# Sums and squares of the last row group in PSUM, with refitted last load sizes, in a streamed sum of squared differences

## The chip, the cores and the metric

One core of a Trainium2 chip. The metric is the device time in microseconds (us) of one execution; inputs lie in HBM, the result goes back to HBM. Most executions of one kernel agree within about 0.3%. A span is the length of one profiled execution; times inside a trace count from its start, which is the issue of the first load.

Three engines matter. SyncE (SP) issues the transfers (DMA), VectorE (DVE) subtracts, ScalarE (ACT) squares and sums. SBUF and PSUM are two memories of the core; the program chooses for each tensor in which of them it lies (`alloc_sbuf_tensor`, `alloc_psum_tensor`).

## The reference

```python
x, y: float32 [1024, 4096]
out = np.sum((x - y) ** 2, axis=-1)        # float32 [1024]
```

Each of the 128 partitions holds 8 consecutive rows, so row group r (called row r) is columns 4096 r to 4096 r + 4095 of a 128 x 32768 matrix. 33.55 MB are read once.

## The kernel before: the parts concerned

The widths of the loads (`xw` of X, `yw` of Y), all issued by SyncE, in columns; each Y load is issued after the X loads that it needs:

```python
xw = [4096, 12288, 8192, 5472, 1280, 960, 320, 160]
yw = [16256, 8192, 2624, 2784, 1344, 480, 480, 288]
late, last = 128, 192        # last: the end of row 7; late: the last 128 columns of row 3, loaded last of all
halved = (1, 2, 3, 4)        # these Y loads are computed in two halves per row
```

For each piece VectorE subtracts in place and ScalarE squares in place; `accum_out` gives a second ScalarE instruction, READ_ACCUMULATOR, which writes the piece's sum into one column of `parts` (for a row in one piece, straight into `results`):

```python
def sub(c0, c1):
    a = X[:, home(c0, c1)]
    nc.vector.tensor_sub(out=a, in0=a, in1=Y[:, home(c0, c1)]).then_inc(diffs, 1)

def square(c0, c1, acc):
    a = X[:, home(c0, c1)]
    nc.scalar.wait_ge(diffs, n["diffs"])
    nc.scalar.activation(out=a, in_=a, func=Square, accum_out=acc).then_inc(acts, 1)
```

A row in several pieces is completed by a VectorE reduction of its columns of `parts`. The last load (the end of row 3) is squared and summed on VectorE itself, while ScalarE does the last piece of row 7. In the traces this sum is CUSTOM_DVE_ANT_0, followed by VectorE's own DVE_READ_ACCUMULATOR2_ANT. The code (cut):

```python
for j, (c0, c1) in enumerate(ys):
    final = j == len(ys) - 1
    wait_loaded(c1, landed_y[j][1])
    for piece in pieces_of(j, c0, c1):
        sub(*piece)
        if final:
            # tensor_tensor_reduce on VectorE, its initial value the first part of row 3
            ...
        square(*piece, where[piece])
        ...
    if j == 4:
        for r in (4, 5, 6):
            complete(r)
complete(7)                   # VectorE waits for ScalarE's last sum, reduces 8 numbers
nc.sync.wait_ge(sums, n["sums"])
nc.sync.dma_start(out=ov, in_=results)
```

Of the kernel before, what the change touches and what calls it, by code (L numbers as in the profile page):

```python
# [47 lines left out]
def kernel(tc, x, y, axis, out):  # L48
    nc = tc.nc
    P = nc.NUM_PARTITIONS  # L50
    F32 = mybir.dt.float32
    Square = mybir.ActivationFunctionType.Square
# [3 lines left out]
    R = B // P  # L56
# [11 lines left out]
    results = nc.alloc_sbuf_tensor("results", [P, R], F32).ap()  # L68



    xw = [4096, 12288, 8192, 5472, 1280, 960, 320, 160]
    yw = [16256, 8192, 2624, 2784, 1344, 480, 480, 288]
    late, last = 128, 192
    LATE = 3
    halved = (1, 2, 3, 4)
    cut = (LATE + 1) * D - late
# [16 lines left out]
    acts = prog.semaphore("acts")  # L94
# [3 lines left out]
    def home(c0, c1):  # L98
        h0 = c0 % H
        return slice(h0, h0 + c1 - c0)  # L100
# [25 lines left out]
    row_parts = [[] for _ in range(R)]  # L126
# [16 lines left out]
    parts, where = None, {}  # L143
    total = sum(len(p) for p in row_parts if len(p) > 1)
    parts = nc.alloc_sbuf_tensor("parts", [P, total], F32).ap()
    k = 0
    for r, p in enumerate(row_parts):
        for piece in p:
            where[piece] = parts[:, k : k + 1] if len(p) > 1 else results[:, r : r + 1]
            k += len(p) > 1  # L150
    first = {}
    k = 0
    for r, p in enumerate(row_parts):
        if len(p) > 1:
            first[r] = k
            k += len(p)

    def parts_of(r, m):
        return parts[:, first[r] : first[r] + m]

    seen_x = [0]

# [15 lines left out]
    def square(c0, c1, acc):  # L178
        a = X[:, home(c0, c1)]
        nc.scalar.wait_ge(diffs, n["diffs"])  # L180
        nc.scalar.activation(out=a, in_=a, func=Square, accum_out=acc).then_inc(acts, 1)  # L181
        n["acts"] += 1

    squared = {}
# [1 line left out]
    def complete(r):  # L186
        nc.vector.wait_ge(acts, squared[row_parts[r][-1]])
        nc.vector.tensor_reduce(  # L188
            out=results[:, r : r + 1],
            in_=parts_of(r, len(row_parts[r])),  # L190
            axis=mybir.AxisListType.X,
            op=add,
        ).then_inc(sums, 1)
        n["sums"] += 1
# [6 lines that stand above are left out]
            r = piece[0] // D  # L201
            if final:
                nc.vector.wait_ge(diffs, n["diffs"])
                nc.vector.tensor_tensor_reduce(  # L204
                    out=Y[:, home(*piece)],
                    in0=X[:, home(*piece)],
                    in1=X[:, home(*piece)],
                    scale=1.0,
                    scalar=parts_of(r, 1),
                    op0=mult,  # L210
                    op1=add,
                    accum_out=results[:, r : r + 1],
                ).then_inc(sums, 1)
                n["sums"] += 1
                continue
            square(*piece, where[piece])
            squared[piece] = n["acts"]
            if r in (0, 1):

                nc.sync.wait_ge(acts, n["acts"])  # L220
                while todo and todo[0][5] <= H + (r + 1) * D:
                    load(*todo.pop(0))
                if r == 1:
                    while todo:
                        load(*todo.pop(0))
# [43 lines left out]
```

## Time and profile before

| | before |
|---|---|
| time, median of the first 3 runs (range) | 84.03 us (84.0 to 84.2) |
| span of the profiled run | 82.6 us |
| DMA engines busy | 95.9% of the span |
| DVE / ACT busy | 45% / 40% |
| last reduction starts / ends | 80.99 / 81.15 us |

How to read it: the 16 DMA engines are busy for nearly the whole span and data arrives until about 79.85 us, so the time is the stream plus a tail. The lines stand in the prediction below. In what follows "landing" is the time of the last of the 16 semaphore updates that the trace records for a load. The load before the last (192 columns before, 160 after) landed at 80.052 us before.

### The profile page before, as it was taken

The page shows a single profiled execution, that of the slowest core. Times are in us where ns is not written, and L with a number is a line of the kernel's source. Part 1 is how long each engine was busy: PE and PEld are TensorE (multiplying, and loading weights), DVE is VectorE, ACT ScalarE, POOL GpSimd, SP SyncE. Part 2 cuts the span into 40 slices and gives each one's busy share as a digit, 9 for nine tenths or more (in the row PEclk, how much of TensorE's full clock was granted, in tenths as well). Part 3 has the DMA queues.
Part 4 walks back from the last instruction along what each step waited for, and adds up shares of the span by engine and source line. Part 5 has one row for each costly group of instructions (what it writes and reads, how often), then busy time and mean ns, then how long its engine had stood idle before and what let it go on. Part 6 is the DMA issues. An engine that isn't in the chain of part 4 may idle for free.

```text
span 82.6 us, 136 instructions
## 1 busy us (share of the span) xinstructions
DVE 36.8 (45%) x27; ACT 33.4 (40%) x41; POOL 0.2 (0%) x4
## 2 busy tenths in 40 slices
DVE  0000000000000000000299999999189996989992
ACT  3300000000000000000000979889896999899991
POOL 0000000000000000000000000000000000000000
DMA  5998998888999991999599699969979799999960
GB/s 127 389 500 381 595 547 381 381 381 381 504 504 504 504 504 63 441 504 504 254 508 508 286 476 508 476 286 508 423 339 509 339 437 440 426 402 416 395 220 2
DMA packets 2736, 33.56 MB, mean 406 GB/s; under 512 B 432, under 2 KB 1328, under 8 KB 1712
## 3 DMA queue, kind: packets, MB, share of 16 engines
q1 hardware_dynamic: 2736, 33.56, 95.9%
HBM read 33.55 MB, written 0.00 MB: 406 GB/s over the span
## 4 chain that ended last, share of the span: by engine, by line
DMA 63%; SPq 16%; DVE 12%; ACT 4%; issue 1%
DMA Y<-in_y_dram 63%; SPq L108 16%; DVE X L175 11%; ACT X L181 4%; DVE Y L204 0%; DVE results L188 0%; SPq L220 0%; DVE results L204 0%
## 5 line engine op out<-in xcount | busy, mean ns | idle before, releaser
L175 DVE TENSOR_TENSOR X<-X,Y 128x2048 f32<-128x2048 f32 (+10 forms) x21 | 36.2, 1780 | 44.3 <-DMA Y<-in_y_dram 44.3
L181 ACT ACTIVATE X<-X 128x2048 f32<-128x2048 f32 (+9 forms) x20 | 31.2, 1559 | 46.1 <-DVE X L175 46.0
L181 ACT ACTIVATION_READ_ACCUMULATOR X<-X 128x1 f32 x20 | 3.7, 186 | 0.0
L181 ACT ACT_TABLE_LOAD x1 | 1.3, 1283 | 1.4 <-PEq L19 1.4
L188 DVE TENSOR_REDUCE results<-parts 128x1 f32<-128x2 f32 (+2 forms) x4 | 0.4, 152 | 0.0
L204 DVE CUSTOM_DVE_ANT_0 Y<-X,parts 128x128 f32<-128x128 f32 x1 | 0.4, 352 | 0.0
L250 POOL MEMSET const-bfloat16-1.0<- 128x1 bf16 x1 | 0.1, 101 | 0.0
L250 POOL MEMSET const-uint8-127<- 128x1 uint8 x1 | 0.1, 101 | 0.0
L250 POOL MEMSET const-float32-0.0<- 128x1 f32 x1 | 0.1, 98 | 0.2 <-issue 0.2
L250 POOL MEMSET const-float32-1.0<- 128x1 f32 x1 | 0.1, 98 | 0.0
L204 DVE DVE_READ_ACCUMULATOR2_ANT results<- 128x1 f32 x1 | 0.1, 83 | 0.0
## 6 DMA issues: line engine op xcount, KB each, us to landing
Y<-in_y_dram SPq DMA_DIRECT2D x1, 8128.0 KB, 39.0
X<-in_x_dram SPq DMA_DIRECT2D x1, 6144.0 KB, 20.2
X<-in_x_dram SPq DMA_DIRECT2D x1, 4096.0 KB, 48.3
Y<-in_y_dram SPq DMA_DIRECT2D x1, 4096.0 KB, 57.5
X<-in_x_dram SPq DMA_DIRECT2D x1, 2736.0 KB, 13.3
X<-in_x_dram SPq DMA_DIRECT2D x1, 2048.0 KB, 7.1
Y<-in_y_dram SPq DMA_DIRECT2D x1, 1392.0 KB, 19.0
Y<-in_y_dram SPq DMA_DIRECT2D x1, 1312.0 KB, 16.1
```

The source lines that it names most:

```text
L108: nc.sync.dma_start(out=dst[:, home(c0, c1)], in_=src[:, c0:c1]).then_inc(sem, 16)
L175: nc.vector.tensor_sub(out=a, in0=a, in1=Y[:, home(c0, c1)]).then_inc(diffs, 1)
L181: nc.scalar.activation(out=a, in_=a, func=Square, accum_out=acc).then_inc(acts, 1)
L188: nc.vector.tensor_reduce(out=results[:, r : r + 1], in_=parts_of(r, len(row_parts[r])), axis=mybir.AxisListType.X, op=add,).then_inc(sums, 1)
L204: nc.vector.tensor_tensor_reduce(out=Y[:, home(*piece)], in0=X[:, home(*piece)], in1=X[:, home(*piece)], scale=1.0, scalar=parts_of(r, 1), ...
L250: nc = _bacc.Bacc("TRN2", target_bir_lowering=False, num_devices=1)
```

## The change

Intent: ScalarE writes row 7's squares and sums to PSUM instead of SBUF, to make each piece take less time, and the last loads are cut again to fit. The diff (cut):

```diff
-    xw = [4096, 12288, 8192, 5472, 1280, 960, 320, 160]
-    yw = [16256, 8192, 2624, 2784, 1344, 480, 480, 288]
-    late, last = 128, 192
+    xw = [4096, 12288, 8192, 5472, 1344, 640, 576, 160]
+    yw = [16256, 8192, 2656, 2816, 1344, 640, 288, 288]
+    late, last = 128, 160
...
+    last_parts = nc.alloc_psum_tensor("last_parts", [P, 512], F32).ap()
+    last_squares = nc.alloc_psum_tensor("last_squares", [P, 7 * 512], F32).ap()
+    squares_at = {}
+    # from the last piece of row 7 backwards, as many as fit
+    for piece in reversed(row_parts[-1]):
+        w = piece[1] - piece[0]
+        if k + w > 7 * 512:
+            break
+        squares_at[piece] = last_squares[:, k : k + w]
+        k += w
...
     def parts_of(r, m):
-        return parts[:, first[r] : first[r] + m]
+        home_of = last_parts if r == R - 1 else parts
+        return home_of[:, first[r] : first[r] + m]
...
-        nc.scalar.activation(out=a, in_=a, func=Square, accum_out=acc).then_inc(acts, 1)
+        to = squares_at.get((c0, c1), a)
+        nc.scalar.activation(out=to, in_=a, func=Square, accum_out=acc).then_inc(acts, 1)
```

Row 7 has 8 pieces on either side: 640, 672, 672, 672, 480, 480, 288, 192 before; 672, 704, 672, 672, 640, 288, 288, 160 after. All 8 sums go to PSUM, and the squares of the last 7 pieces. PSUM is touched by ScalarE alone until VectorE's reduction, which waits for ScalarE's last sum.

More of the change, by code (lines that the diff above doesn't have):

```diff
@@ L145 @@
     parts = nc.alloc_sbuf_tensor("parts", [P, total], F32).ap()
+    last_parts = nc.alloc_psum_tensor("last_parts", [P, 512], F32).ap()
+    last_squares = nc.alloc_psum_tensor("last_squares", [P, 7 * 512], F32).ap()
+    squares_at = {}
     k = 0
-    for r, p in enumerate(row_parts):
-        for piece in p:
-            where[piece] = parts[:, k : k + 1] if len(p) > 1 else results[:, r : r + 1]
-            k += len(p) > 1
+    for piece in reversed(row_parts[-1]):
[4 more added lines that the diff above has]
+        k += w
     first = {}
@@ L154 @@
         if len(p) > 1:
-            first[r] = k
-            k += len(p)
+            first[r] = 0 if r == R - 1 else k
+            k += 0 if r == R - 1 else len(p)
     def parts_of(r, m):
-        return parts[:, first[r] : first[r] + m]
+        home_of = last_parts if r == R - 1 else parts
+        return home_of[:, first[r] : first[r] + m]
+    for r, p in enumerate(row_parts):
+        for k, piece in enumerate(p):
+            where[piece] = parts_of(r, len(p))[:, k : k + 1] if len(p) > 1 else results[:, r : r + 1]
     seen_x = [0]
```

## The prediction

> **What bounds the kernel now.** I read the page first: the DMA row of the slices, the queue share and the chain that ended last.
>
> ```profile
> DVE 36.8 (45%) x27; ACT 33.4 (40%) x41; POOL 0.2 (0%) x4
> DMA  5998998888999991999599699969979799999960
> q1 hardware_dynamic: 2736, 33.56, 95.9%
> DMA 63%; SPq 16%; DVE 12%; ACT 4%; issue 1%
> ```
>
> Both compute engines are idle more than half of the span; the 16 DMA engines are busy for 95.9% of it, and the row of slices runs on into slice 39. (The single 1 there is bookkeeping of long packets, not a hole: by the list of DMA issues and the chain, the first long X load lands at 1.43 + 20.2 = 21.6 us and the first long Y load, 8128 KB = 8.32 MB, at 40.84 us, which is 433 GB/s without a pause.) The 33.55 MB that must be read is the same in both kernels. So the kernel is the stream of loads plus a tail, and only the tail can move. The table by stretches shows where the stream stops (columns: stretch, its length, DVE busy, ACT busy, POOL busy, clock, DMA share, GB/s):
>
> ```profile
> 74.00:76.00 2.00, 2.00 (x4) 2.00 (x7) 0.00 (x0) 1.00 1.01 417
> 76.00:78.00 2.00, 2.00 (x4) 2.00 (x5) 0.00 (x0) 1.00 1.02 405
> 79.60:79.70 0.10, 0.10 (x1) 0.10 (x1) 0.00 (x0) 1.00 1.05 305
> 79.80:79.90 0.10, 0.10 (x1) 0.10 (x1) 0.00 (x0) 1.00 0.08 16
> 79.90:80.00 0.10, 0.10 (x1) 0.10 (x2) 0.00 (x0) 1.00 0.00 0
> ```
>
> Data ends near 79.85 us; VectorE (DVE) and ScalarE (ACT) have been full since 74. The three have been balanced against each other. Next the chain in order of time (columns: start, length, what):
>
> ```profile
> 66.94 13.12 DMA Y<-in_y_dram
> 80.08 0.57 DVE X L175 x2
> 80.67 0.35 DVE Y L204
> 81.03 0.12 DVE results L188
> ```
>
> The timeline (columns: start, length, engine, line, operation, destination and sources):
>
> ```profile
> 79.47 0.59 ACT L181 ACTIVATE X<-X 128x480 f32<-128x480 f32 x1
> 79.58 1.06 DVE L175 TENSOR_TENSOR X<-X,Y 128x288 f32<-128x288 f32 x3 [0.15 <-DMA Y<-in_y_dram]
> 80.08 0.44 ACT L181 ACTIVATE X<-X 128x288 f32<-128x288 f32 x1
> 80.42 0.19 ACT L181 ACTIVATION_READ_ACCUMULATOR X<-X 128x1 f32 x1
> 80.52 0.35 ACT L181 ACTIVATE X<-X 128x192 f32<-128x192 f32 x1
> 80.77 0.19 ACT L181 ACTIVATION_READ_ACCUMULATOR X<-X 128x1 f32 x1
> 80.95 0.08 DVE L204 DVE_READ_ACCUMULATOR2_ANT results<- 128x1 f32 x1
> 80.99 0.16 DVE L188 TENSOR_REDUCE results<-parts 128x1 f32<-128x8 f32 x1
> 81.18 0.35 SPq L232 DMA_DIRECT2D out_dram<-results  x1
> ```
>
> Two paths meet at the last reduction of row 7. DVE: the 192-column load lands at 80.05, subtraction at 80.08, the 128 late columns of row 3 are subtracted and summed by 80.95, their accumulator is read by 81.03. ACT: its last piece can only start at 80.52, because the pieces before it fill it, and its accumulator is out at 80.96. The reduction starts at 80.99, within 0.04 us of both, ends at 81.15, and the store takes the rest up to 82.6. The whole tail after the last-but-one landing, up to the start of the reduction, is 80.99 - 80.05 = 0.94 us. The measured time, 84.03 us, is the span plus about 1.4 us.
>
> **What the Trainium skill says.** "PSUM — Partial Sum Buffer" (Specifications, engine access) says ScalarE writes PSUM faster than SBUF. "Perfetto Trace Analysis" (Optimizing Scalar/DVE Operations) gives sizes: about 93 ns of access overhead for ScalarE on SBUF against 51 on PSUM, and about 60 against 125 for VectorE. The before trace has no PSUM operand, so it can't confirm either. "ScalarE: Activation LUTs" (What ACT_TABLE_LOAD costs) gives 186 ns + 0.833 ns per column for an ACTIVATE with immediate operands; the trace agrees: 192 columns took 347 ns (formula 346), 672 took 754 (746). "DMA: Bandwidth & Descriptors" (Where 436 GB/s comes from) puts the ceiling at 435 GB/s; 433 above agrees, so the stream has nothing left to give.
>
> **The change part by part.** By the order of instructions, every engine has as many instructions on both sides: 20 ACTIVATEs, 21 subtractions, 18 loads and the store. No wait is added or removed.
>
> *Loads.* As many descriptors (18 loads of 128 rows) and the same bytes, so the fixed cost per packet is paid equally often and the stream ends where it did, 79.85 us. The last two Y loads (160 and 128 columns instead of 192 and 128) still land about 80.05 and 80.25. Effect: 0, with phase noise of maybe 0.1 us.
>
> *DVE's last pieces.* In the trace the 192-column subtraction holds DVE for 0.28 us before the next (80.08 to 80.36, the start of a 285 ns instruction that ends at 80.65), that is 0.20 for 192 columns at 1.04 ns (slope from 2048 and 4096 columns: (4421 - 2287)/2048) and 0.08 fixed. With 160 columns it starts the next at 80.08 + 0.167 + 0.08 = 80.33, after the landing at 80.25, so row 3's end comes 0.033 us sooner: its sum starts near 80.64 and lets go of DVE near 80.95 to 80.96.
>
> *ACT's shorter pieces.* From start to start a piece costs ACT its columns at 0.833 plus about 0.20 us (672 columns: 78.11 to 78.88 = 0.77; 480: 78.88 to 79.47 = 0.59). The new cut gives ACT of row 7 two 288s, a 160, a 640 and 704 in place of 480, 480, 288, 192 and 640. I walked this queue with landings shifted by the columns that follow. With the old 0.20 it would start the last 160 at about 80.73 and have its sum out near 81.14, that is 0.18 later than now: **the new sizes alone would lose**. With 0.04 us less per piece (estimate, 93 - 51 ns, from the page "Perfetto Trace Analysis") it reaches the 640 before its subtraction is done, starts it at 79.10, then 79.80, 80.20 and 80.60, and is out near 80.93. With 0.08 (both instructions of a piece gaining) 80.83. So PSUM pays for the new cut; it does not add a gain of its own beyond the DVE bound of 80.95.
>
> *The reduction.* It now reads its 8 numbers from PSUM: +0.065 us at most (estimate, 125 - 60 ns, same page) on the path that ends last; the before kernel's reduction took 0.16.
>
> Sum on the path: start of the reduction 80.99 to about 80.96 (-0.03), its length +0.00 to +0.065. Net -0.03 to +0.03 us of 84.03: nothing that a median of three can hold.
>
> **The rivals.** (1) *ACT was the real bound of the tail* and is relieved by much more than I took: then the end follows DVE, and cannot be earlier than the last landing plus two subtractions and the sum; at best -0.1 us, 83.93. For: ACT has no gap from 74 to 81. Against: DVE is equally full and ends within 0.04 us of it. (2) *PSUM writes save ACT no time between pieces* (only the acknowledgement that already overlaps the next instruction gets shorter): then the finer cut makes ACT late, +0.1 to +0.18 us, 84.15 to 84.2. For: READ_ACCUMULATOR's 186 ns already overlap the next ACTIVATE by half (80.42 + 0.19 against a start at 80.52). Against: the cut was evidently fitted to something shorter. (3) *The stream shifts*: the new starting columns change how rows are cut, for 0.1 us either way. Before and after have about equally many such small loads, so I give it noise only. (4) Collisions in PSUM: ACT alone writes there, and DVE reads only after ACT's last semaphore, so none.
>
> **Range and chances.** Centre: 84.03 - 0.03 to + 0.03, pulled down slightly by rival 1, gives 83.98. The three old runs span 84.0 to 84.2, so medians wander by some 0.1; with the +0.18 of rival 2 and stream noise of 0.1 I take 83.78 to 84.2. A 2% gain is 1.68 us, more than the 0.94 us tail that could be touched, so faster gets 0.01; a 2% loss needs the stream to slow from 433 to about 424 GB/s, which nothing here does, 0.01.
>
> **What would show it.** In the profile after: the DMA share still 95 to 96% and the last waited-for landing at 80.0 to 80.1; a 160-column subtraction followed by the 128 one about 0.25 us later; ACTIVATEs with PSUM outputs with a fixed part of about 0.14 instead of 0.19 us, pieces following each other at 0.833 per column plus 0.12 to 0.16 instead of 0.20; ACT's last sum out at 80.8 to 80.95; the reduction of 128x8 starting near 80.96 and taking 0.16 to 0.23 us. I am wrong if the stream ends more than 0.2 us elsewhere, if ACT's pieces keep their 0.20 and the reduction starts after 81.1, or if ACT had held DVE back earlier by something that I don't see.

## The result and the profile after

| | before | after |
|---|---|---|
| time, median of 6 (range) | 84.13 us (84.0 to 84.2) | 84.09 us (83.97 to 84.38) |
| ratio, 95% interval | | 1.0001 (0.9983 to 1.0019) |
| span of the profiled run | 82.6 us | 82.8 us |
| landing of the load before the last | 80.052 us | 80.136 us |
| last reduction starts, us after that landing | 0.936 | 0.976 |

A ratio is the mean time of one kernel's runs over that of the other's of the same rounds, so not quite the ratio of the medians quoted. The page of after:

```profile
DVE 36.8 (45%) x27; ACT 33.2 (40%) x41; POOL 0.2 (0%) x4
q1 hardware_dynamic: 2736, 33.56, 95.9%
DMA 70%; DVE 17%; ACT 7%; issue 1%; SPq 1%
```

The DMA share is 95.9% in both. ACT does 0.2 us less work in all (33.4 before). The table by stretches of after (stretch, length, DVE, ACT, POOL busy, clock, DMA share, GB/s) has the stream's end where it was, within a tenth:

```profile
76.00:78.00 2.00, 2.00 (x3) 2.00 (x7) 0.00 (x0) 1.00 1.03 407
79.80:79.90 0.10, 0.10 (x1) 0.10 (x2) 0.00 (x0) 1.00 0.32 87
79.90:80.00 0.10, 0.10 (x1) 0.10 (x3) 0.00 (x0) 1.00 0.04 10
```

The chain of waits of after, in order of time (start, length, what), no longer leads through a landing of the tail:

```profile
54.46 18.97 DMA Y<-in_y_dram
73.45 1.63 DVE X L186 x2
...
78.20 0.28 DVE results L200 x3
78.48 0.74 DVE X L186
79.24 1.85 ACT last_squares L193 x8
81.11 0.17 DVE results L200
```

Before, it ran through the DMA up to 80.05 us. Now it leaves the DMA at 73.43, runs through VectorE up to the 640-column subtraction, with the three reductions of rows 4 to 6 in the middle, and then through ScalarE's last four pieces. The timeline of after shows these (start, length, engine, line, operation, destination and source):

```profile
79.24 0.71 ACT L193 ACTIVATE last_squares<-X 128x640 f32<-128x640 f32 x1
...
80.32 0.41 ACT L193 ACTIVATE last_squares<-X 128x288 f32<-128x288 f32 x1
80.65 0.14 ACT L193 ACTIVATION_READ_ACCUMULATOR last_squares<-X 128x1 f32 x1
80.70 0.32 ACT L193 ACTIVATE last_squares<-X 128x160 f32<-128x160 f32 x1
80.93 0.15 ACT L193 ACTIVATION_READ_ACCUMULATOR last_squares<-X 128x1 f32 x1
81.00 0.08 DVE L216 DVE_READ_ACCUMULATOR2_ANT results<- 128x1 f32 x1
81.11 0.17 DVE L200 TENSOR_REDUCE results<-last_parts 128x1 f32<-128x8 f32 x1
```

Two things to see. From the start of READ_ACCUMULATOR to that of the next ACTIVATE it is 0.05 us here (80.65 to 80.70); before it was 0.09 (80.424 to 80.517). And the reduction starts 0.033 us after ScalarE's sum is out (81.079), while VectorE's own READ_ACCUMULATOR began at 81.00: ScalarE is last.

### The profile page after: what moved, and what is told of

Read it like the earlier page. It is cut to its first block, busy times and chain, and to the rows that moved or that the text cites. A ratio compares the mean times of both kernels' runs of the same rounds, so it can differ in the third digit from the quotient of the medians.

```text
span 82.8 us, 136 instructions
## 1 busy us (share of the span) xinstructions
DVE 36.8 (45%) x27; ACT 33.2 (40%) x41; POOL 0.2 (0%) x4
## 3 DMA queue, kind: packets, MB, share of 16 engines
q1 hardware_dynamic: 2736, 33.56, 95.9%
## 4 chain that ended last, share of the span: by engine, by line
DMA 70%; DVE 17%; ACT 7%; issue 1%; SPq 1%
DMA Y<-in_y_dram 70%; DVE X L186 16%; ACT X L193 4%; ACT last_squares L193 2%; SPq L108 1%; DVE results L200 1%; SPq L232 0%
## 5 line engine op out<-in xcount | busy, mean ns | idle before, releaser
L186 DVE TENSOR_TENSOR X<-X,Y 128x2048 f32<-128x2048 f32 (+11 forms) x21 | 36.2, 1780 | 44.4 <-DMA Y<-in_y_dram 44.3
L193 ACT ACTIVATE X<-X 128x2048 f32<-128x2048 f32 (+7 forms) x13 | 26.9, 2072 | 46.3 <-DVE X L186 46.2
L193 ACT ACTIVATE last_squares<-X 128x672 f32<-128x672 f32 (+4 forms) x7 | 4.0, 582 | 0.1
L193 ACT ACTIVATION_READ_ACCUMULATOR X<-X 128x1 f32 x13 | 2.4, 184 | 0.0
L193 ACT ACTIVATION_READ_ACCUMULATOR last_squares<-X 128x1 f32 x7 | 0.9, 134 | 0.0
```

Of the source, the lines that this page charges most:

```text
L193: nc.scalar.activation(out=to, in_=a, func=Square, accum_out=acc).then_inc(acts, 1)
```

## The experiments

The theory: the stream of loads fixes the time. PSUM saves ScalarE a fixed time per piece, and the new cut of the last loads spends it again. Rivals: PSUM saves no time between pieces; or ScalarE's tail is the whole story and its relief should show; or the engines' tail holds more than the 0.94 us that I read.

### The sizes alone: e1_sizes_only

```diff
 # the kernel before, with the new numbers only
-    xw = [4096, 12288, 8192, 5472, 1280, 960, 320, 160]
-    yw = [16256, 8192, 2624, 2784, 1344, 480, 480, 288]
-    late, last = 128, 192
+    xw = [4096, 12288, 8192, 5472, 1344, 640, 576, 160]
+    yw = [16256, 8192, 2656, 2816, 1344, 640, 288, 288]
+    late, last = 128, 160
```

> The new sizes with all of row 7 left in SBUF. My theory: ScalarE's pieces keep about 0.19 to 0.20 us of fixed cost from start to start, so after the 640-column piece the three last pieces come 0.04 to 0.05 us later each than in the changed kernel and the last accumulator is out 0.15 us later: the last reduction starts about 81.25 us, 1.1 us after the landing of the 160-column load (0.98 in the changed kernel, 0.94 before). Time 84.2 to 84.3, ratio to before 1.001 to 1.002, at the edge of the noise; the trace decides. Rival (the sizes alone are harmless, PSUM pays for nothing): the reduction starts 0.94 to 0.98 us after that landing.

Measured: 84.23 us against 84.11, ratio 1.002 (1.0007 to 1.0032), so slower by 0.2%. The timeline of its tail:

```profile
79.22 0.74 ACT L181 ACTIVATE X<-X 128x640 f32<-128x640 f32 x1
...
80.97 0.08 DVE L204 DVE_READ_ACCUMULATOR2_ANT results<- 128x1 f32 x1
81.03 0.19 ACT L181 ACTIVATION_READ_ACCUMULATOR X<-X 128x1 f32 x1
81.25 0.16 DVE L188 TENSOR_REDUCE results<-parts 128x1 f32<-128x8 f32 x1 [0.20 <-ACT X L181]
```

VectorE waits 0.20 us for ScalarE. From the start of the 640-column ACTIVATE to the start of the reduction it is 81.248 - 79.217 = 2.031 us, in the changed kernel 81.112 - 79.242 = 1.870. The reduction starts 1.143 us after the landing (80.105). So PSUM is worth 0.16 us in the new cut. Against the kernel before, the new cut alone starts the reduction 0.21 us later from the landing (1.143 against 0.936), and the times show a loss as well (+0.12 us of medians).

### PSUM alone: e2_psum_only

```diff
 # the changed kernel, with the old numbers
-    xw = [4096, 12288, 8192, 5472, 1344, 640, 576, 160]
-    yw = [16256, 8192, 2656, 2816, 1344, 640, 288, 288]
-    late, last = 128, 160
+    xw = [4096, 12288, 8192, 5472, 1280, 960, 320, 160]
+    yw = [16256, 8192, 2624, 2784, 1344, 480, 480, 288]
+    late, last = 128, 192
```

> Row 7 in PSUM with the old sizes. My theory: ScalarE's last piece ends its accumulator about 0.1 us earlier than before, but VectorE's sum of row 3's end lets go only at about 0.94 us after the landing of the 192-column load, so the reduction starts there: no gain, ratio 1.000 within 0.002. Rival (ScalarE alone sets the tail): the reduction starts 0.84 us after that landing, time 0.1 us shorter.

Measured: 84.13 us against 84.11, ratio 1.0001 (0.9989 to 1.0014). The timeline:

```profile
81.01 0.13 ACT L193 ACTIVATION_READ_ACCUMULATOR last_squares<-X 128x1 f32 x1
81.18 0.08 DVE L216 DVE_READ_ACCUMULATOR2_ANT results<- 128x1 f32 x1
81.18 0.16 DVE L200 TENSOR_REDUCE results<-last_parts 128x1 f32<-128x8 f32 x1
```

The reduction starts at the same nanosecond as VectorE's READ_ACCUMULATOR, 0.898 us after the landing (80.285), not the 0.94 that I expected. So VectorE was free to reduce 0.04 us earlier than the kernel before did: there READ_ACCUMULATOR began at 80.950 and the reduction at 80.988, that is 0.031 after ScalarE's sum (80.957). ScalarE, not VectorE, held the end before, by 0.04 us. The other traces bear this out: in after, e1, e10 and e12 the reduction starts 0.032 to 0.033 us after ScalarE's sum, as it did before (0.031), and in e7, e9 and e11 at the same nanosecond as VectorE's READ_ACCUMULATOR. In e2 ScalarE's sum is out 0.862 us after the landing (81.147) instead of 0.905 before, so 0.04 earlier and not the 0.1 that I expected, and again 0.036 before the reduction, so the two engines tie in this run, whose landing came 0.23 us later than before's; a run with an earlier landing might be held by ScalarE. The gain that PSUM alone can have in the tail is this 0.04 us, too little for the times to show.

### The fixed cost magnified: e3_fine_sbuf, e4_fine_psum, e5_fine_sums_psum, e6_fine_squares_psum

Row 7 cut into 67 pieces, 61 of 64 columns and 6 of 32 (the expectations say 66), so that ScalarE becomes the bound:

```diff
-        return pieces
+        fine = []
+        for c0, e in pieces:
+            step = 64 if c0 // D == R - 1 else e - c0
+            fine += [(c, min(c + step, e)) for c in range(c0, e, step)]
+        return fine
```

e3 has this in SBUF (the kernel of e1), e4 in the changed kernel. e5 puts only the sums in PSUM (`to = a`), e6 only the squares (`home_of = parts`, and row 7's columns counted with the others).

> Only to magnify the fixed cost: row 7 cut into 66 pieces of at most 64 columns, all in SBUF, new sizes. ScalarE becomes the bound from about 76 us on. With 0.19 us per piece and 62 columns at 0.833 ns in the mean: 66 x 0.245 = 16.2 us, so about 95.4 us of time. Correct result.

> The same 66 pieces with the accumulators in PSUM and the squares of the last 56 or so in PSUM. If PSUM takes 0.05 us off each piece from start to start, as the last three pieces of the changed kernel show (0.143 instead of 0.19 fixed): 66 x 0.195 = 12.9 us, about 92.1 us of time, 3.3 us less than the SBUF version. Rival (only the acknowledgement that overlaps anyway gets shorter): the same time as the SBUF version within 0.3 us.

> The 66 small pieces with the accumulators alone in PSUM, the squares in SBUF. Theory A (the time between pieces is freed by where READ_ACCUMULATOR writes: in the full version the step from ACTIVATE to READ_ACCUMULATOR is 0.146 us either way for 64 columns and only the step from READ_ACCUMULATOR to the next ACTIVATE falls from 0.093 to 0.051): pieces every 0.197 us as in the full version, time 92.7. Theory B (the destination of the squares frees it): every 0.239 us as in SBUF, time 95.2.

> The 66 small pieces with the squares alone in PSUM, the accumulators in SBUF. Theory A (accumulator's destination): pieces every 0.239 us, time 95.2. Theory B (destination of the squares): every 0.197 us, time 92.7. If the growing durations of the full version (8 ns more at each piece) are a queue of writes to PSUM, they show in the one of the two versions that makes it and not in the other.

| | squares | sums | time, us | median step of a 64-column piece, ns | ACTIVATE to READ_ACCUMULATOR, ns |
|---|---|---|---|---|---|
| e3_fine_sbuf | SBUF | SBUF | 95.18 | 238 | 146 |
| e4_fine_psum | PSUM | PSUM | 92.69 | 197 | 146 |
| e5_fine_sums_psum | SBUF | PSUM | 92.81 | 197 | 146 |
| e6_fine_squares_psum | PSUM | SBUF | 95.01 | 238 | 146 |

(A step is from the start of one ACTIVATE to that of the next.) All four are correct. The two with sums in PSUM are 2.2 to 2.5 us faster than the two without. The destination of the squares changes neither the step nor, beyond 0.2 us, the time. ScalarE's timelines of e3, e6 and e5, in this order:

```profile
87.02 0.24 ACT L185 ACTIVATE X<-X 128x64 f32<-128x64 f32 x1
87.16 0.19 ACT L185 ACTIVATION_READ_ACCUMULATOR X<-X 128x1 f32 x1
87.25 0.24 ACT L185 ACTIVATE X<-X 128x64 f32<-128x64 f32 x1
```

```profile
86.89 0.20 ACT L197 ACTIVATE last_squares<-X 128x64 f32<-128x64 f32 x1
87.03 0.19 ACT L197 ACTIVATION_READ_ACCUMULATOR last_squares<-X 128x1 f32 x1
87.13 0.20 ACT L197 ACTIVATE last_squares<-X 128x64 f32<-128x64 f32 x1
```

```profile
86.61 0.68 ACT L197 ACTIVATE X<-X 128x64 f32<-128x64 f32 x1
86.75 0.59 ACT L197 ACTIVATION_READ_ACCUMULATOR X<-X 128x1 f32 x1
86.80 0.69 ACT L197 ACTIVATE X<-X 128x64 f32<-128x64 f32 x1
```

Squares in PSUM (e6) make the ACTIVATE itself read shorter, 0.20 instead of 0.24 us, but the next instruction starts no sooner. Sums in PSUM (e5) bring the next ACTIVATE 0.05 us after READ_ACCUMULATOR instead of 0.09. That is theory A, and it settles which half of the change pays.

One more thing shows only here. In e4 and e5 the durations grow by 8 ns at each piece, for READ_ACCUMULATOR from 0.15 us to 0.67 (e4) and 0.68 (e5), while the starts stay 0.197 us apart: the ends fall behind the starts. The last sum counts, so of 0.041 us saved per piece some 0.034 is left: from the first ACTIVATE of 64 columns to the last end it is 15.916 us in e3 and 13.648 in e4, and (15.916 - 13.648)/67 = 0.034. The ends are real to the rest of the program: the last reduction starts 0.032 us after the recorded end of the last sum in both. Why they fall behind was not tested. It goes with the sums and not with the squares, since e6 doesn't show it. It accounts for most of why I expected 92.1 us for e4 and got 92.69: the 66 x 0.05 us that I had reckoned is rather 67 x 0.034.

### Two reductions out of the way: e7_reductions_early

```diff
-        if j == 4:
-            for r in (4, 5, 6):
-                complete(r)
+        if j == 2:
+            for r in (4, 5):
+                complete(r)
+        if j == 4:
+            complete(6)
```

> The changed kernel with the reductions of rows 4 and 5 moved to where VectorE waits for the load before row 6's end. My theory: in the changed kernel VectorE is busy without a gap from the landing at 73.4 us to the 640-column subtraction, and ScalarE's last four pieces follow that; 0.125 us less there let ScalarE end about 0.12 us sooner, so the last reduction starts 0.90 to 0.94 us after the landing of the 160-column load instead of 0.98. Time 0.04 to 0.08 us less, ratio to before 0.999 to 1.000, not to be told from 1. Rival (ScalarE's end follows the landings): 0.98 us as in the changed kernel.

Measured: 84.04 us against 84.14, ratio 0.9996 (0.9976 to 1.0017), correct. The timeline:

```profile
79.14 0.71 ACT L193 ACTIVATE last_squares<-X 128x640 f32<-128x640 f32 x1
...
81.02 0.08 DVE L216 DVE_READ_ACCUMULATOR2_ANT results<- 128x1 f32 x1
81.02 0.16 DVE L200 TENSOR_REDUCE results<-last_parts 128x1 f32<-128x8 f32 x1
```

ScalarE's four pieces start 0.1 us earlier, and now VectorE is the last again: the reduction starts 0.862 us after the landing (80.162) instead of 0.976. The trace follows the theory, a little beyond the range given for it; the times can't tell it from nothing.

### What the tail could give at most: e9_both_light

The edits (cut):

```diff
+        if c0 >= N - 1376 or c0 == cut:      # in sub: the last five loads
+            c1 = c0 + 32
...
+        if c0 >= N - 1376:                   # in square
+            c1 = c0 + 32
...
+                piece = (piece[0], piece[0] + 32)     # VectorE's sum of row 3's end
```

> Wrong result on purpose: the changed kernel with only 32 columns of each of the last five loads' pieces computed on either engine; all loads unchanged. It measures what the tail could give at most. My theory: the stream ends as ever, the last reduction starts about 0.63 us after the landing of the 160-column load instead of 0.98 and the time falls by some 0.35 us, ratio about 0.996; a gain of 2% isn't there to be had. Rival (the engines' tail holds more than I read, or the loads wait for the engines somewhere): ratio below 0.99.

Measured: 83.8 us against 84.14, ratio 0.9962 (0.9946 to 0.9979); the result is wrong on purpose. The chain of waits (start, length, what) leads straight from the landing to the end:

```profile
67.21 13.06 DMA Y<-in_y_dram
80.30 0.19 DVE X L188
...
80.72 0.25 DVE Y L222
```

The reduction starts at 80.897, 0.622 us after the landing. Taking away most of the arithmetic of the last five loads gains 0.4%. Even all of the 0.94 us from the landing to the reduction would be 1.1% of 84 us, so nothing that is done to these pieces can reach 2%.

### Sums alone in the real cut: e10_sums_only, e11_sums_only_early, and the changed kernel again: e12_after_again

e10 is the changed kernel with `to = a` (squares stay in SBUF), e11 is e7 with the same edit, e12 is the changed kernel unedited.

> The changed kernel with only the sums of row 7 in PSUM, the squares in SBUF. If the destination of the sums is all that frees ScalarE, pieces of the tail follow READ_ACCUMULATOR by 0.05 us as in the changed kernel and the last reduction starts about 0.98 us after the landing of the 160-column load; time within 0.2% of before. Rival (squares matter in the real cut): back to the 1.14 us of the sizes alone, 84.25 us.

> Sums alone in PSUM and the reductions of rows 4 and 5 early, the cheapest version that the runs point to. Expected: the last reduction starts 0.86 to 0.90 us after the landing of the 160-column load (0.86 with squares in PSUM as well, where VectorE was the bound), time 0.05 to 0.1 us below the changed kernel in the mean, ratio to before 0.999 to 1.000, not to be told from 1.

> The changed kernel once more on the chip of these runs, for a second trace: the last reduction should again start 0.96 to 1.0 us after the landing of the 160-column load with ScalarE's accumulator last, whatever the landing's own time; ratio to before 1.000 within 0.002.

| | time, us | ratio to before (95%) | last reduction after the landing, us | 640-column ACTIVATE to last reduction, us |
|---|---|---|---|---|
| before (first trace) | 84.16 in these rounds | | 0.936 | |
| e12_after_again | 84.12 | 0.9990 (0.9973 to 1.0008) | 0.978 | 1.870 |
| e10_sums_only | 84.20 | 1.0003 (0.9986 to 1.0020) | 0.926 | 1.898 |
| e11_sums_only_early | 84.06 | 0.9995 (0.9972 to 1.0018) | 0.864 | 1.946 (ends on VectorE) |

e12 repeats the changed kernel's tail to the nanosecond (1.870 us again), while the landing itself lay elsewhere. In e10 I expected 0.98 and got 0.926: the landing came late in that trace (80.410), so the measure from the landing is a poor one where ScalarE's queue, started earlier, sets the end. Measured along ScalarE's own queue, e10 is 0.03 us longer than e12 and 0.13 shorter than e1 (2.031). Squares in PSUM are therefore worth 0.03 us in the real cut, sums 0.13. The timeline of e10:

```profile
79.44 0.74 ACT L193 ACTIVATE X<-X 128x640 f32<-128x640 f32 x1
...
81.13 0.18 ACT L193 ACTIVATION_READ_ACCUMULATOR X<-X 128x1 f32 x1
81.34 0.17 DVE L200 TENSOR_REDUCE results<-last_parts 128x1 f32<-128x8 f32 x1
```

This agrees with e6, where the squares did not change the step: in e10 the starts from the 640-column ACTIVATE to the last READ_ACCUMULATOR are 1.688 us apart, in e12 1.687. The 0.03 us is the last READ_ACCUMULATOR alone, 0.178 us long here and 0.151 in e12. The 0.13 us of the sums is three steps of 0.041 and 0.009 in that last instruction (0.187 us in e1). e11 ends on VectorE, 0.86 us after the landing as expected. It has the shortest tail together with e7, and by its time it is not to be told from before or after: no version here beats both kernels.

## Why the prediction was right

The prediction was the same time, 83.98 us in 83.78 to 84.2; measured 84.09, ratio 1.0001. Step by step:

- *The stream is fixed.* Right. The DMA share is 95.9% on both sides, the data ends within 0.1 us of where it did, and e9 gains 0.4% with hardly any arithmetic left in the tail. The prediction's comparison with 435 GB/s carries less than it reads: the section that it cites works this figure out for the ports into SBUF, not for loads from HBM.
- *The new sizes alone would lose 0.18 us.* Right: in e1 ScalarE's last sum is out 1.111 us after the landing, before 0.905, so 0.21 later, and the time is 1.002 of before.
- *0.04 us less per piece with PSUM.* Right in size: 0.041 from start to start in the magnified runs. Wrong in its place: I gave it to the ACTIVATE's fixed part, from 0.19 to 0.14 us. In the changed kernel that part is 0.17 (640 columns in 707 ns), and the time between pieces comes from READ_ACCUMULATOR's destination alone. Where pieces follow each other closely, the growing ends take 0.008 us per piece back.
- *ScalarE's walk, 79.10, 79.80, 80.20, 80.60, out at 80.93.* The spacing was about right (0.70, 0.40, 0.40, 0.33; measured 0.70, 0.38, 0.38, 0.38), the start 0.14 us early: ScalarE's sum was out at 81.08, outside the 80.8 to 80.95 named as a sign, and the reduction started at 81.112, just past the 81.1 given as a sign of being wrong, though not with the 0.20 us per piece that was to go with it. The load at whose landing the chain leaves the DMA came at 73.43 instead of 73.25. Hardly any of this is the change's doing. The first load of the program, the same in both kernels, already landed 0.15 us later in the trace of after (7.267 against 7.117 us); from `--dma`, before and then after, the last number being us from issue to landing:

```profile
X<-in_x_dram SPq DMA_DIRECT2D x1, 2048.0 KB, 7.1
X<-in_x_dram SPq DMA_DIRECT2D x1, 2048.0 KB, 7.3
```

With 0.15 us taken off, the walk starts at 79.09 and its sum is out at 80.93, as predicted. That the end fits so closely is luck: the two middle steps were 0.02 us shorter each than foreseen and the last piece 0.05 longer, which cancels. With the old cut this load landed at 73.25 in one trace and at 73.53 in another (e2), with the new one between 73.34 and 73.62. Such shifts reach the span: after and e12 are the same kernel, their landings before the last differ by 0.058 us and their spans by 0.057.

- *VectorE holds the end.* Wrong, both before and after. The chain of before named VectorE, which ended within 0.04 us of ScalarE; e2, e7 and e11 show that the reduction can start together with VectorE's READ_ACCUMULATOR, so ScalarE held the end by 0.04 us before and by 0.11 us after (81.00 to 81.11). VectorE's own share was read well: its READ_ACCUMULATOR starts 0.863 us after the landing instead of 0.898, 0.035 sooner where 0.033 was predicted. Taking the wrong engine cost nothing because both were so near and the whole tail is so short; in that the number was lucky.
- *The reduction from PSUM, up to 0.065 us more.* Not there: 0.167 instead of 0.161 us, and it starts 0.033 instead of 0.031 us after ScalarE's sum.
- *Net -0.03 to +0.03 us.* From the landing to the reduction's end it is 1.097 us before and 1.143 after, so +0.05 in the pair of traces, slightly outside. From the first load's landing to the reduction's start it is 73.871 us before, 73.845 after and 73.854 in e12, so -0.02 to -0.03, inside. The sign depends on where one starts to count, so the tail's net change is not told from zero, by the traces or by the times.

Still open: why sums written to PSUM end later and later, and whether the 0.1 us that e7 and e11 win in the trace is a gain in time at all (their intervals hold 1).

## What to carry to other kernels

Before a tail is tuned, add up how long it is from the last landings to the last reduction: here 0.94 us of 84, so that no tuning of it could reach 2% (the reduction and the store after it took another 1.63 to 1.64 us in each of these traces). A saving per piece and a new cut that spends it each need a test alone, else a useful part and a harmful part show as nothing. Where two engines end within some 0.05 us of each other, the chain's name for the last one is not to be trusted; see what the reduction starts with when one of them is relieved. Before times of 0.1 us are compared between two traces, compare something that the change cannot touch, as the first load's landing here.

## What the Trainium skill lacked or had wrong

- "ScalarE: Activation LUTs" (What ACT_TABLE_LOAD costs) gives the cost of an ACTIVATE, 186 ns + 0.833 ns per column, and an overlap of about 93 ns, but not that of the sum: with an accumulator each piece has a second instruction of 186 ns, and the step of 64 columns is 238 ns, that is 53 + 185 (e3).
- "PSUM — Partial Sum Buffer" (Specifications) calls PSUM the faster destination for ScalarE and doesn't say for which of the two outputs of an ACTIVATE with a sum. The squares' destination changed the step by 0 ns (e6: 238), the sums' by 41 (e5: 197); where the sums lie in PSUM, moving the squares there as well shortened the last READ_ACCUMULATOR from 178 to 151 ns (e10, e12). The figures 93 and 51 ns of "Perfetto Trace Analysis" (Optimizing Scalar/DVE Operations) fit the time from READ_ACCUMULATOR to the next ACTIVATE, 0.093 and 0.051 us.
- No page tells that small sums written to PSUM back to back end later and later, 8 ns at each piece, from 0.15 up to 0.68 us for a READ_ACCUMULATOR after 67 of them (e5).
- "Perfetto Trace Analysis" (same section) has VectorE's overhead at about 125 ns on PSUM and 60 on SBUF. In the reduction of 8 numbers per partition, read from PSUM or SBUF and written to SBUF, no such difference showed: 167 against 161 ns. The page doesn't say whether reading alone counts.
